# Transposes that nobody reads in TensorE's waits: a two-block model with experts on one core

## Chip, cores and metric

The kernel runs on one core of a Trainium2 chip. The metric is the device time of one execution in microseconds (us); lower is better. A profiled execution gives the trace: what each engine did and when, what ended each wait, and the clock that was granted to TensorE.

## What is computed

2048 tokens of width 1024 go through two blocks, all in float32. Cut to its steps:

```python
# first block
h = rmsnorm(x) * (1 + sc1) + sh1
q_a, k_a, v_a, q_h, f_h, i_h, g_h = split(h @ w_in)
mix = concat(window_attention(q_a, k_a, v_a), hgrn(q_h, f_h, i_h) * silu(g_h)) @ w_out
x = x + ga1 * rmsnorm(mix)
h = rmsnorm(x) * (1 + sc2) + sh2
g = top1(softmax(h @ w_rg)); e = top2(softmax(h @ w_re within g))     # 4 groups of 8 experts
y = sum over the 2 experts of weight * (silu(h @ gate) * (h @ up)) @ down
x = x + ga2 * rmsnorm(y)
# second block
xn = rmsnorm(x)
qa, ka, va, ga, qb, kb, vb, gb, iq, ik, iw, za, zb = split(xn @ w_in_2)
ya = chunked_attention(qa, ka, va, rel_bias) * silu(ga)               # 64-token chunks, 8 chunks back
yb = sparse_attention(rope(qb), rope(kb), vb, top256(index(iq, ik, iw))) * silu(gb)
out = rmsnorm(x + (sigmoid(za) * (ya @ w_branch_a) + sigmoid(zb) * (yb @ w_branch_b)) @ w_out_2)
```

## The kernel before

Every matrix product of float32 data is made from three products of halves: an operand is split into a high part (names ending in hi or h, rounded to the type float32r, mostly by ScalarE) and a low part (lo or l, the rest, by VectorE), and TensorE sums hi x hi, lo x hi and hi x lo in a PSUM bank. Activations must be transposed before that; TensorE does it by a product with an identity (`ident`) into PSUM, in groups of four 128x128 tiles in one bank.

`build` (L3062) runs five stages one after the other.

- `P1`: projections, window attention and the HGRN recurrence, to about 910 us.
- `P2` (L1127): for each of 16 blocks of 128 tokens (`unit`, L1243) the output projection (`pA`, `pS`, three products each), the two norms, the store of the new tokens to X1 and H2, 8 transposes of h, 16 router products into `pU` (tile `hT` by `wr`), and the choice of experts, a chain of small VectorE operations from the logits `lg` on. After the last block comes the table that says which tokens each expert gets (`cnt`, `order`, `base`, `gidx`; tiles `sa`, `sv`, `tab`, `perm`). To about 1168 us.
- `MoE` (L1514): 48 tiles of gathered tokens in an order written out by hand. POOL gathers four tiles ahead (`gather`, tile `xg`), `xT` transposes one, `gu` makes gate and up, `down` the rest. `W.split` splits the weights that SP's queue brings. To about 1639 us.
- `Overflow` (L1689): VectorE works out whether an expert got more tokens than the tiles hold, in `ovi`; every engine loads that value into a register (L1710) and branches on it (L1711). The body isn't run with these inputs.
- `S3` (L1858), the second block. Its first part (`run`, L2878) takes each token block in through `Combine`: POOL gathers two experts' rows (`cy`), SP loads X1 (`cx`), `finish` (L1833) weighs, sums, norms (sum of squares `css`, tile `ss`) and adds them; `norm_block` (L1949) norms again (`nss`, also `ss`), transposes and splits; and `proj` (L1988) starts the projections, 128x256 or 128x512 products into `pA`, with `rot` and `st` behind them on POOL, VectorE and ScalarE. The weights come on SP's queue into one staging buffer `ld`; ScalarE rounds them (`whi`, `whix`) and VectorE takes the rest (`wlo`). Then follow both attentions with more projections as filler, and the tail.

**What sets the order.** Except in `MoE` and `Overflow`, the program's order on each engine comes out of a plan that is made while it is built. `Clock` (L35) holds a time for each engine and each tile, with costs from formulas (`cost`, L135: a transpose 0.109 us, a gather 1.04 on POOL, and in the call 0.65 + 1.46 + 0.95 more to landing). Work is written as generators (lanes); `B.on` lets one go on once its engine and its tiles are planned to be free. `B.run` (L320) takes the first lane that can issue something, and where none can it steps the plan's time:

```python
            if state:
                idle = 0
                continue
            c.now += 0.05
            idle = idle + 1 if state is BLOCK else 0
```

The engines then run their instructions in that order, and wait for each other by semaphores. The plan isn't told how long things take on the chip. Nearly all instructions are recorded through one helper, so the trace puts them on line L122; they are told apart by their tiles. PSUM has eight banks, two for each of the names pA, pS, pT, pU; a bank is "open" in the plan from its allocation to `done`.

Of the kernel before, what the change touches and what calls it, by code (L numbers as in the profile page):

```python
# [34 lines left out]
class Clock:  # L35
# [3 lines left out]
    def __init__(self):  # L39
        self.t = dict.fromkeys(("tensor", "vector", "scalar", "gpsimd", "sync", "dma"), 0.0)  # L40
        self.ready, self.last, self.by, self.free = {}, {}, {}, {}
        self.now, self.open = 0.0, set()
# [8 lines left out]
    def op(self, eng, outs, ins, cost, lat=0.0, far=0.0):  # L51
        t = self.t[eng]
        for a in ins:
            n = a.tensor.name
            t = max(t, self.ready.get(n, 0.0) + (0.12 if self.by.get(n) != eng else 0.06))
        for a in outs:
            n = a.tensor.name
            t = max(t, self.free.get(n, 0.0))
            if self.by.get(n) != eng:
                t = max(t, self.last.get(n, 0.0))  # L60
        if eng == "sync":
            self.t[eng] = t + 0.05
            d = self.t["dma"] = max(self.t["dma"], t + 1.1) + cost
            end = d + 0.95
        else:
            self.t[eng] = t + cost
            end = t + cost + lat
            if far:
                d = self.t["dma"] = max(self.t["dma"], t + cost + 0.65) + far
                end = d + 0.95  # L70
        for a in ins:
            n = a.tensor.name
            self.last[n] = max(self.last.get(n, 0.0), end)
        for a in outs:
            n = a.tensor.name
            self.ready[n] = max(end, self.ready.get(n, 0.0)) if self.by.get(n) != eng else end
            self.last[n] = max(self.last.get(n, 0.0), end)
            self.by[n] = eng
        return t

# [127 lines left out]
class B:  # L208


    def __init__(self, tc, ctx, I):
# [4 lines left out]
        self.sm = None  # L216
        self.spawned, self.lanes = [], []
# [26 lines left out]
    def bank(self, *tags):  # L244

        while True:
            for tag in tags:
                slots = self.ps.slots.get(tag)
                if slots is None or any(x not in self.clock.open for x in slots):
                    return (yield from self.ps.get([128, 512], F32, tag, bufs=2))  # L250
            yield BLOCK

# [65 lines left out]
    def run(self, *lanes, back=(), first=()):  # L318
# [6 lines left out]
        while lanes or self.spawned:  # L325
# [15 lines left out]
            if state:  # L341
                idle = 0
                continue
            c.now += 0.05
# [782 lines left out]
class P2:  # L1127
# [336 lines left out]
    def run(self):  # L1464
        b = self.b
        st, en = b.phase("p2")
        with st:
# [3 lines left out]
            self.lg, self.perm = {}, None  # L1471
            b.run(pipe(self.units(), 4), self.mix_lane(range(4, NTB), self.P, "mraw", 2, self.P, "msq", b.rsqrt2))

# [40 lines left out]
class MoE:  # L1514
# [129 lines left out]
    def run(self):  # L1644
        st, en = self.b.phase("mo")
        with st:
            self.setup(en)
            W, NT = self.W, self.NT
            for t in range(4):
                self.gather(t)  # L1650
            W.split(3)
# [37 lines left out]
class Overflow:  # L1689
# [5 lines left out]
    def run(self):  # L1695
        b, nc, tc = self.b, self.nc, self.b.tc
        st, en = b.phase("ov")
        with st:
# [10 lines left out]
            nc.vector.tensor_copy(mi, mx)  # L1709
            v = nc.values_load(mi[0:1, 0:1], min_val=0, max_val=T)  # L1710
# [96 lines left out]
class Combine:  # L1807
# [11 lines left out]
    def block(self, blk, then=None):  # L1819
# [10 lines left out]
        yield from b.load(x, self.X1[blk * 128:blk * 128 + 128, :])  # L1830
        b.spawn(self.finish(blk, x, *ys, then))

    def finish(self, blk, x, y1, y2, then):  # L1833
# [7 lines left out]
        self.started = True  # L1841
        r = yield from b.rsqrt2(ss, 1, 1.0 / D, "cr")
# [15 lines left out]
class S3:  # L1858
# [90 lines left out]
    def norm_block(self, x, blk, hi, lo):  # L1949
# [4 lines left out]
        b.done(jk)  # L1954
        y = yield from b.rsqrt2(ss, 1, 1.0 / D, "nr")
# [885 lines left out]
    def run(self):  # L2841
# [18 lines left out]
        with self.b.pool("s_k") as c:  # L2860
            self.consts(c)
            self.keys(c)
            with ExitStack() as st:
# [4 lines left out]
                with b.pool("s_ro") as c:  # L2868
# [3 lines left out]
                    with b.pool("s_c") as self.C:  # L2872
# [4 lines left out]
                        self.W.extra, self.W.hi_eng = (self.C, range(3, 6)), "scalar"  # L2877
                        b.run(self.norm_lane(), self.proj(0, range(8), groups=True), self.const_lane(), first=b.lanes)  # L2878
                    fill = chain(self.proj(0, range(8, 32), last=True), self.xn_load(2), self.xn_load(3), self.proj(1, range(12), groups=True))
# [218 lines left out]
```

## Time and profile before

| | us |
|---|---|
| Median of 3 runs | 4056.64 |
| The runs | 4056.0, 4056.64, 4059.93 |
| Profiled execution | 4061.26 |
| Its span, first to last instruction | 4059.4 |
| TensorE (PE) busy | 3646.1 (90%) |
| VectorE (DVE) busy | 2734.8 (67%) |
| ScalarE (ACT) busy | 2283.2 (56%) |
| GpSimd (POOL) busy | 901.4 (22%) |
| Mean granted TensorE clock | 0.951 |

The trace belongs to one execution, the profiled one; 1.86 us of it lie outside the span. Times within the trace are us from the span's start. A granted clock of 1.00 is TensorE at 2.4 GHz, 0.50 is 1.2 GHz. Busy time of a matmul is from its issue to its modelled end, so neighbours overlap: in a row of like ones the distance of two starts is the price of one. PE stands for matmuls and transposes, PEld for weight loads, PEldq for the queue's own instructions, SP for the engine that issues most transfers.

### The profile page before, as it was taken

To read this page: it belongs to the slowest core of one execution; us is meant where nothing else is said; L and a number is where in the kernel's file an instruction comes from. 1 tells how busy PE (TensorE), PEld (TensorE's weight loads), DVE (VectorE), ACT (ScalarE), POOL (GpSimd) and SP (SyncE) were. 2 spreads that over 40 slices of the span, in tenths; PEclk is the share of its full clock that TensorE was granted. 3 is DMA by queue.
4 is the path that set the end of the run, shared out by engine and by line. 5 is a ranking of instruction groups with operands and counts; after the bars stand their busy time and mean duration, and the time that the engine had idled before them with its cause. 6 is when DMAs were issued, how large, how long until landed. Compare 5 with 4: busy or idle time off the path is not lost.

```text
span 4059.4 us, 64576 instructions
## 1 busy us (share of the span) xinstructions
PE 3646.1 (90%) x21649; PEld 3167.4 (78%) x21649; DVE 2734.8 (67%) x7027; ACT 2283.2 (56%) x4628; POOL 901.4 (22%) x1650
## 2 busy tenths in 40 slices
PE   3999999979969999397999989999889988999997
PEld 2888788768858888296777779888678877999997
DVE  7866785697777777526366743467766656878772
ACT  3654655565546666424257755357667774676751
POOL 1310000031011100473044526111033321211110
PEclk9999999979989999598999989999889998999999
DMA  6233451125358887739887773543166527787767
GB/s 229 79 108 110 137 198 60 64 81 167 130 202 314 314 315 285 263 126 339 290 255 249 249 283 108 169 147 101 43 187 180 173 81 270 259 281 272 265 230 283
DMA packets 425744, 801.28 MB, mean 197 GB/s; under 512 B 129360, under 2 KB 245296, under 8 KB 424496
## 3 DMA queue, kind: packets, MB, share of 16 engines
q1 hardware_dynamic: 407472, 748.70, 54.3%
q0 software_dynamic: 17920, 48.26, 3.5%
q8 instruction: 176, 2.88, 0.3%
q14 instruction: 176, 1.44, 0.1%
HBM read 571.02 MB, written 234.18 MB: 198 GB/s over the span
## 4 chain that ended last, share of the span: by engine, by line
PE 37%; DMA 7%; POOL 4%; DVE 3%; issue 3%; ACT 2%; SPq 1%; POOLq 0%; DVEq 0%; ACTq 0%
PE pA L122 22%; PE pS L122 5%; PE pT L122 5%; PE pU L122 5%; POOL rot L122 1%; DMA x<-IQ 1%; SPq L122 1%; DMA x<-QB 1%; DMA tz<-TZ 1%; POOL st L122 1%; DMA Q<-QA 0%; DMA sg<-SG 0%; DVE scb L122 0%; DVE pp L122 0%; POOL QB L122 0%
## 5 line engine op out<-in xcount | busy, mean ns | idle before, releaser
L122 PE MATMUL pA<-xnl,whi 128*128 128x512 f32 x1024 | 415.3, 406 | 5.4 <-DVE st L122 5.4
L122 DVE TENSOR_TENSOR wlo<-ld,whi 128x1024 fp32r<-128x1024 f32 x271 | 328.7, 1243 | 112.6 <-ACT whi L122 74.8
L122 PE MATMUL pA<-xnh,wlo 128*128 128x512 f32 x1024 | 403.7, 394 | 0.4 <-DVE wlo L122 0.4
L122 PE MATMUL pA<-xnh,whi 128*128 128x512 f32 x1024 | 403.9, 394 | 0.0
L122 DVE TENSOR_TENSOR pp<-pT,pp 128x256 fp32r<-128x256 f32 (+1 forms) x568 | 295.1, 537 | 117.5 <-ACT pp L122 113.8
L122 ACT ACTIVATE pp<-pT 128x256 fp32r<-128x256 f32 (+1 forms) x568 | 260.6, 478 | 201.5 <-PE pT L122 189.3
L122 PE MATMUL pA<-hlo,whi 128*128 128x512 f32 x832 | 352.1, 423 | 10.0 <-issue 6.7
L122 PE MATMUL pA<-hhi,wlo 128*128 128x512 f32 x832 | 328.8, 395 | 0.0
L122 PE MATMUL pA<-hhi,whi 128*128 128x512 f32 x832 | 327.9, 394 | 0.0
L122 ACT ACTIVATE whi<-ld 128x1024 fp32r<-128x1024 f32 x212 | 213.5, 1052 | 59.0 <-PE pA L122 35.3
L122 DVE SCALAR_TENSOR_TENSOR acc<-rl,iw,acc 128x512 f32<-128x512 f32 (+3 forms) x304 | 220.8, 727 | 38.0 <-ACT rl L122 31.4
L122 PEld LDWEIGHTS pA<-xnh,wlo 128*128 128x128 f32 x1024 | 193.9, 189 | 44.8 <-DVE wlo L122 1.1
L122 ACT ACTIVATE bias<-acc,sst 128x1152 f32<-128x1152 f32 (+13 forms) x168 | 220.0, 1309 | 13.3 <-DVE sst L122 9.6
L122 PEld LDWEIGHTS pA<-xnl,whi 128*128 128x128 f32 x1024 | 195.4, 191 | 33.6 <-issue 5.8
L122 PE MATMUL pA<-wlo,xnh 128*128 128x256 f32 (+1 forms) x672 | 200.9, 299 | 22.2 <-DVE st L122 12.4
L122 PEld LDWEIGHTS pA<-xnh,whi 128*128 128x128 f32 x1024 | 194.9, 190 | 29.4
L122 PE MATMUL pU<-pp,vbS 128*128 128x256 f32 x1088 | 203.2, 301 | 10.2 <-DVE pp L122 8.3
L122 ACT ACTIVATE rl<-pS 128x512 f32<-128x512 f32 (+3 forms) x304 | 163.6, 544 | 82.4 <-PE pS L122 42.9
L122 PE MATMUL pA<-whi,xnl 128*128 128x256 f32 (+1 forms) x672 | 197.5, 294 | 4.1 <-DMA xnl<-XND 4.1
L122 PE MATMUL pA<-whi,xnh 128*128 128x256 f32 (+1 forms) x672 | 197.6, 294 | 0.0
L122 ACT ACTIVATE st<-pA 128x256 f32<-128x256 f32 (+4 forms) x160 | 73.6, 460 | 202.6 <-PE pA L122 161.5
L122 PEld LDWEIGHTS pA<-hlo,whi 128*128 128x128 f32 x832 | 159.4, 192 | 35.9 <-issue 9.4
(494 smaller groups left out, 11117.2 us busy)
## 6 DMA issues: line engine op xcount, KB each, us to landing
whi<-W2P SPq DMA_DIRECT2D x172, 512.0 KB
wlo<-W2P SPq DMA_DIRECT2D x172, 512.0 KB
ld<-in_w_gu_dram SPq DMA_DIRECT2D x128, 512.0 KB
ld<-in_w_dn_dram SPq DMA_DIRECT2D x64, 512.0 KB
W2P<-whi SPq DMA_DIRECT2D x57, 512.0 KB
W2P<-wlo SPq DMA_DIRECT2D x57, 512.0 KB
Y<-ym SPq DMA_DIRECT2D x48, 512.0 KB
xl<-in_wadaT_dram SPq DMA_DIRECT2D x32, 512.0 KB
```

Source lines behind the costliest of these rows:

```text
L122: r = real(*a, **k)
```

## The change

While TensorE is planned to be idle it is given transposes of the identity into a PSUM bank that nobody reads. There are two kinds.

*Fixed groups*, in `turn`: 48 after the first four gathers of `MoE.run` (L1644), 56 before the register load of `Overflow.run` (L1710), and three by `turn_at` in the first token block of the second block: 56 once X1's rows have landed (`Combine.block`, L1819), 48 after the first sum of squares (`Combine.finish`, L1833) and 40 after the second (`S3.norm_block`, L1949). `turn_at` puts a one-column matmul on the tile in front, so that the group waits for it.

*Bursts of three*, in `idle_turn`: where `B.run` finds nothing to issue and steps its time, it adds three transposes if TensorE has been idle for over 0.2 us in the plan, was planned busy for less than 60% of the last stretch (`share`), and a PSUM bank is free and was last used over 0.5 us ago. This is switched on (`turning`) in `P2.run` (L1464) and in the first part of `S3.run` (L2878), which goes from about 1643 to 2000 us.

All of it enters the plan as TensorE time, so what is planned behind it may take another order.

```diff
--- before.py
+++ after.py
@@ class Clock
+        self.pe = []
...
             end = t + cost + lat
+            if eng == "tensor":
+                self.pe.append((t, t + cost))
...
+    def share(self, span=3.4):
+
+        a = self.now - span
+        while self.pe and self.pe[0][1] <= a:
+            self.pe.pop(0)
+        return sum(min(y, self.now) - max(x, a) for x, y in self.pe if x < self.now) / span
...
@@ class B
+        self.turning = False
...
+    def turn(self, n, after=None):
+
+        c, s = self.clock, self.ps.slots
+        tag = min((c.last.get(x, 0.0), tag) for tag in s for x in s[tag] if x not in c.open)[1]
+        t = yield_value(self.ps.get([128, 512], F32, tag, bufs=2))
+        if after is not None:
+            self.nc.tensor.matmul(t[:, 0:1], self.ident, after, start=True, stop=True)
+        for k in range(n):
+            self.nc.tensor.transpose(t[:, k % 4 * 128:(k % 4 + 1) * 128], self.ident, self.ident)
+        self.done(t)
+
+    def idle_turn(self):
+
+        c, s = self.clock, self.ps.slots
+        if self.turning and c.t["tensor"] < c.now - 0.2 and c.share() < 0.6:
+            if any(x is not None and x not in c.open and c.last.get(x, 0.0) < c.now - 0.5 for y in s.values() for x in y):
+                self.turn(3)
+
+    def turn_at(self, after, n):
+
+        yield from self.on("tensor", after)
+        self.turn(n, after)
+        yield 1
...
             if state:
                 idle = 0
                 continue
+            self.idle_turn()
             c.now += 0.05
...
@@ P2.run
+            b.turning = True
             b.run(pipe(self.units(), 4), self.mix_lane(range(4, NTB), self.P, "mraw", 2, self.P, "msq", b.rsqrt2))
+            b.turning = False
...
@@ MoE.run
             for t in range(4):
                 self.gather(t)
+            b = self.b
+            b.turn(48)
             W.split(3)
...
@@ Overflow.run
             nc.vector.tensor_copy(mi, mx)
+            b.turn(56)
             v = nc.values_load(mi[0:1, 0:1], min_val=0, max_val=T)
...
@@ Combine.block
         yield from b.load(x, self.X1[blk * 128:blk * 128 + 128, :])
+        if blk == 0:
+            b.spawn(b.turn_at(x[:, 0:1], 56))
         b.spawn(self.finish(blk, x, *ys, then))
...
@@ Combine.finish
         self.started = True
+        if blk == 0:
+            b.spawn(b.turn_at(ss, 48))
...
@@ S3.norm_block
         b.done(jk)
+        if blk == 0:
+            b.spawn(b.turn_at(ss, 40))
...
@@ S3.run
+                        b.turning = True
                         b.run(self.norm_lane(), self.proj(0, range(8), groups=True), self.const_lane(), first=b.lanes)
+                        b.turning = False
```

## Rows read from the trace of the kernel before

**Rows 1.** The page, part 2: granted clock in 40 slices of 101.5 us.

```profile
PEclk9999999979989999598999989999889998999999
```

**Rows 2.** Stretches: us, busy us of each engine, granted clock, DMA share, GB/s.

```profile
1142.10:1179.70 37.60, 12.46 (x53) 10.58 (x54) 25.36 (x78) 11.21 (x16) 7.92 (x5) 0.50 0.45 166
...
1179.70:1184.00 4.30, 4.30 (x20) 3.48 (x19) 4.17 (x4) 2.46 (x3) 0.00 (x0) 1.00 1.02 405
...
1640.50:1719.00 78.50, 18.09 (x78) 16.04 (x79) 49.25 (x115) 34.90 (x62) 42.15 (x36) 0.50 0.85 304
...
1740.00:1832.00 92.00, 92.00 (x782) 92.00 (x782) 19.17 (x45) 24.40 (x70) 67.62 (x246) 1.00 0.36 124
...
1841.90:1848.70 6.80, 6.20 (x29) 6.20 (x30) 5.39 (x7) 0.87 (x1) 2.37 (x1) 0.50 0.83 328
...
1864.00:1932.00 68.00, 50.10 (x298) 44.83 (x297) 41.37 (x79) 28.73 (x52) 19.98 (x12) 0.89 1.03 361
...
1938.00:2000.00 62.00, 62.00 (x283) 51.44 (x282) 17.73 (x23) 13.52 (x20) 0.00 (x0) 1.00 0.86 293
```

**Rows 3.** TensorE's timeline: start, us, operation, count, idle before and its releaser.

```profile
1124.27 0.70 PE L122 MATMUL pU<-sa,sv 128*64 128x128 f32 x8 [1.27 <-DVE sa L122]
...
1128.48 1.87 PE L122 MATMUL pU<-wr,hT 128*128 128x36 f32 x16
...
1135.75 1.03 PE L122 MATMUL pT<-ident,h 128*128 128x128 f32 x8
...
1147.31 1.94 PE L122 MATMUL pT<-ident,h 128*128 128x128 f32 x8 [8.25 <-DVE h L122]
1149.08 3.63 PE L122 MATMUL pU<-wr,hT 128*128 128x36 f32 x16
...
1164.26 1.12 PE L122 MATMUL pU<-sa,sv 128*64 128x128 f32 x8 [1.11 <-DVE sa L122]
...
1175.65 1.97 PE L122 MATMUL pT<-ident,xg 128*128 128x128 f32 x8 [9.24 <-DMA xg<-Y,gidx]
...
1638.11 0.40 PE L122 MATMUL pU<-whi,al 128*128 128x512 f32 x1
1674.99 1.94 PE L122 MATMUL pT<-ident,cx 128*128 128x128 f32 x8 [36.48 <-DVE cry L122]
```

**Rows 4.** Stretches as in rows 2: two with many transposes.

```profile
903.20:906.60 3.40, 1.54 (x9) 1.17 (x9) 3.34 (x15) 1.47 (x4) 0.00 (x0) 1.00 0.14 46
1736.00:1739.40 3.40, 1.58 (x14) 1.58 (x15) 1.91 (x2) 0.88 (x2) 3.22 (x12) 1.00 0.95 388
```

**Rows 5.** TensorE's timeline as in rows 3: the transposes there.

```profile
900.94 2.00 PE L122 MATMUL pT<-ident,sc 128*128 128x128 f32 x8
...
1737.82 1.09 PE L122 MATMUL pT<-ident,cx 128*128 128x128 f32 x8 [2.46 <-DVE cx L122]
```

**Rows 6.** VectorE's timeline: the last unit's router logits.

```profile
1152.75 0.20 DVE L122 TENSOR_TENSOR lg<-pU,rb 128x36 f32<-128x36 f32 x1 [5.59 <-PE pU L122]
```

**Rows 7.** Lines L1710 and L1711 on TensorE's queue: ns, start us.

```profile
L1710 PEldq TENSOR_LOAD <-ovi x1: 1060/1060/1060, 1640.2 to 1640.2; - x1
...
L1711 PEldq COMPARE_BRANCH  x1: 3832/3832/3832, 1641.4 to 1641.4; - x1
```

**Rows 8.** POOL's timeline: the third stage's first gather.

```profile
1646.30 0.98 POOL L122 DMA_INDIRECT cy<-Y,pos  x1 [56.77 <-DMA crow<-ROW]
```

**Rows 9.** The chain of waits, 1600 to 2020 us: start, us, what.

```profile
1823.92 9.57 DMA cy<-Y,pos
...
1842.50 7.29 PE pA L122 x36
...
1856.57 1.95 PE pT L122 x8
1858.52 6.75 PE pA L122 x42
...
1931.73 8.39 PE pA L122 x24
```

## The prediction

> **What bounds the kernel now.** I read the page first: TensorE is busy 90% of the span, and in the line of its granted clock, one digit for each 101.5 us, most are 9 (full), with a 7 in the slice from 812 us, an 8 from 1116, a 5 from 1624 and an 8 from 1827 [rows 1]. The first of these is the end of the first stage, which the change leaves alone; it bears on the other three. The change can only pay where TensorE runs at half clock (1.2 of 2.4 GHz) **and** something waits for it, so next came the table of stretches [rows 2]. The later projections are TensorE-bound at clock 1.00: 92 us busy of 92, 62 of 62. At 0.50 stand the end of the second stage (1142 to 1180, TensorE busy 12.46 of 37.60 us) and the first projections (1640 to 1719, 18.09 of 78.50), where other engines set the pace.
>
> The price of half clock is read from like operations. Eight fp32 transposes take 1.03 us at full and 1.94 at half clock [rows 3], so in a long row about 0.11 and 0.21 each (the last drains in what is over). A 128x256 matmul takes 92.00/782 = 0.118 us [rows 2] and 6.20/29 = 0.214 [rows 2].
>
> Do transposes hold the clock? At 900.94 eight of them run for 2.00 us at half clock, behind a few matmuls; from 903.20 the clock stands at 1.00. And from 1736 it stays at 1.00 over 3.4 us with 1.58 busy, most of it by 8 transposes of 1.09 [rows 4, 5]. That speaks for yes, without proving it for a stretch of transposes alone. The Trainium skill ("TensorE: Matmul & The Clock Gate", Part 4: PE-mode transpose) says the opposite: the gate "doesn't engage" for a transpose, which is not counted as busy in the same way. These rows disagree with it. By it the sum below would be not a gain but the loss of the last rival, about 25 us.
>
> **Part by part.**
>
> *Second stage, bursts of three.* Its middle is full already. In the tail the last router unit waits for its h until 1147.31, then runs 8 transposes (1.94) and 16 router matmuls (3.63) at half clock; VectorE gets lg at 1152.75 after 5.59 us of waiting for just this, and sets the chain from there [rows 3, 6]. At full clock the transposes take 1.03, as at 1135.75. The 16 have one spell at full clock beside other work, 1.87 at 1128.48 [rows 3]. So lg is 0.91 + 1.76 = 2.7 earlier at most; the copy between the two groups doesn't shrink, and I take 2.1. The eight table matmuls at 1164.26 take 1.12 against 0.70, worth 0.4; the short ones on the same chain perhaps 0.35 together. That is -2.85. Against it, a real operation can come up behind a burst: 3 x 0.109 = 0.33 us. Five handovers from VectorE to TensorE in that chain (1147, 1158, 1162, 1164, 1166), each late by 0 to 0.33, cost 0.45 on average luck. **-2.4**, between -2.85 and +1.6 (all five hit, nothing warmer).
>
> *48 before the first expert.* TensorE waits 9.24 us for the gathered tokens until 1175.65 [rows 3]. 48 x 0.11 = 5.3 us fit; then some 4 us are idle again and the clock may have fallen before the tokens land. If it holds, the eight transposes save 0.9, and the 2.1 us from their end to that of the stretch at 0.50, 1179.70 [rows 2], halve, 1.0. But the transfers run at a share of 1.02 from 1179.7 to 1184 [rows 2], where the next experts' weights come in: what is won is waited for there. At half clock 48 x 0.21 = 10.1, or 0.9 late. **0**, bounds -1.9 and +0.9.
>
> *56 before the overflow branch.* The branch isn't taken, but TensorE's queue has to pass it: it reads its register at 1640.2 and its branch takes 3.83 us, to 1645.2 [rows 7], and POOL's first gather issues at 1646.30, behind TensorE's and VectorE's queues [rows 8]. The last expert matmul starts at 1638.11 [rows 3] and ends near 1638.5, so 56 x 0.11 = 6.2 us of transposes end at 1644.7. If the queue's register load waits for the last of them, it moves from 1640.2 to 1644.7: +4.5 on all that follows. If the queue hands the transposes to the array and goes on ahead of it, the cost is 0. Before the change no matmul was outstanding at 1640.2, so no row shows which. I take **+0.8**, near the lower end, as none of the 56 waits for anything and matmuls elsewhere start back to back [rows 3], which asks for some running ahead. Ends 0 and +4.5.
>
> *First projections: 56, 48, 40 and bursts.* TensorE waits 36.48 us until 1674.99 [rows 3]. The three groups are each released by a product of the first token block's own chain, and the last, 40 x 0.11 = 4.4 us, starts some 7 us before the first real transpose, after the norm's sum of squares; it fits. At half clock it would take 8.4 and delay that transpose by about 1.5. From 1675 to 1719 matmuls at half clock are busy 18.09 of the time; VectorE's 49.25 and transfers at 0.85 set the pace [rows 2]. Warm, TensorE's share of the chain (4 transposes and a few matmuls after each norm) shortens by about 0.5. **-0.5**, ends -1.5 and +1.5.
>
> *After the TensorE-bound stretch*, bursts again. In the chain of waits stand four pieces of TensorE at half clock [rows 9]: 36 matmuls 128x256 in 7.29 us, against 36 x 0.118 = 4.25 at full clock, 3.0 to win; 8 transposes 1.95 against 1.03, 0.9; 42 matmuls 6.75 against 4.96, 1.8; 24 of 128x512 in 8.39 against 24 x 62.00/283 = 5.26 by the TensorE-bound stretch behind them [rows 2], 3.1. Together 8.8. Between 1864 and 1932 the transfers' share is 1.03 [rows 2], so what is won earlier can be waited for there. And a burst is only put where the *plan* sees TensorE idle. The plan gives a gather 1.04 + 0.65 + 1.46 + 0.95 = 4.1 us, and at 1823.92 one took 9.57 [rows 9]; the idle behind it is in part unknown to the plan. I count half: **-4.4**, ends 0 and -8.8. Bursts in front of real work, as above but over 360 us, with half of them in idle time: **+0.7**, ends 0 and +4 (a dozen at 0.33).
>
> A burst takes a PSUM bank only where one is free and old, and its transposes read only the identity: no queue of SP or POOL gets an instruction more. What changes there is the order, since every later choice of the plan follows its clocks: 2000 us of work behind this stage may come out in another order. Size and sign are open; the nearest row is the gather of 9.57 us, one slip of which on the chain is the unit. I centre it on 0, ends -6 and +10.
>
> **Sum:** -2.4 + 0 + 0.8 - 0.5 - 4.4 + 0.7 = -5.8 us. The profiled execution has 4061.26 (span 4059.4), 4.6 above the median of 4056.64; it becomes 4055.5, the median **4051**. About 0.2%, 8 us here, is what a measurement can tell from no change.
>
> **Rivals.**
>
> *All of it is won.* The bursts cover the idle as it is, the branch is free, and being early by 8.8 at 1940 stays, since 1938 to 2000 is full TensorE at 1.00: -2.85 - 1.9 - 1.5 - 8.8 = -15, so 4042. For it: pieces of TensorE at half clock lie on the chain. Against: transfers at 1.03. **0.29**, from 4036 to 4048.
>
> *Hidden.* The won time is waited for at the transfers, and the branch's drain takes 4.5: between 4050 and 4062, at 4056. **0.12**.
>
> *Another order.* A transfer of the replanned half lands a group later and TensorE waits twice the 9.57 less the 5.8 won: about +13, 4070; or the loss just eats the gain. **0.12**.
>
> *Slower, by one mechanism: transposes don't hold the clock.* It decides at the first burst after 1142. The bursts fill until 60% of a planned stretch is busy; at half clock each takes 0.64 where the plan has 0.33, so TensorE runs behind. In 1640 to 1719 some 0.6 x 78.5 - 9 = 38 planned us are filled and take 74, with 60 idle there [rows 2]: +14. In the tail 0.6 x 37.6 - 6 = 16.5 become 32, with 25 idle: +7. Add 0.9, 1.5 and the branch's 4.5 or less: **about +25**, 4082. Against it stand the rows at 900 and 1736 [rows 4, 5]; for it, that neither is a stretch of transposes alone. **0.06**. It is the case that the Trainium skill's page, above, would give.
>
> **How the numbers follow.** My own case (half the gain) has 0.41, from 4046 to 4057, and 0.12 of that lies below 4048.5. Faster by over 0.2%: 0.29 + 0.12 = 0.41. Slower: 0.06 from the clock, 0.07 from the order, 0.04 from drain plus bursts: 0.17. The rest, 0.42, is within. The range goes from the far end of the second case, 4036, to 4064, which holds all cases but the slower 0.17 and a few hundredths below it.
>
> **What would show it.** Right: clock 1.00 in the windows from 1147 to 1168, lg some 2 us earlier after h, the first gather at most 1 us later after the last expert matmul, the chain's pieces of 128x256 matmuls at 0.118 each. Wrong: a stretch filled with identity transposes at 0.50 (last rival); a load of the register at 1644 (drain); bursts of three absent from the idle before the matmuls of [rows 9], where the plan didn't see it; or a chain after 2000 whose transfers land later than before.

## The result and the profile after

The changed kernel takes **4105.16 us** (median of four runs, 4104.2 to 4105.36) against 4058.28 for the kernel before beside it: a ratio of 1.0102, 95% interval 1.0082 to 1.0122. That is 47 us slower (41 above the range's upper end, 4064), where 6 us faster had been forecast. A second measurement on another chip, among the experiments, gave 1.0109 (1.0094 to 1.0123).

The page of the changed kernel, its head and the line that answers to [rows 1]:

```profile
span 4103.5 us, 66804 instructions
...
PE 3770.0 (92%) x22767; PEld 3288.9 (80%) x22767; DVE 2729.8 (67%) x7026; ACT 2287.3 (56%) x4630; POOL 891.3 (22%) x1651
...
PEclk9999999979999999999999989999999988999999
```

TensorE got more to do (1118 instructions, 124 us) and its clock did rise: the 5 of the slice from 1624 us and the 8s from 1116 and 1827 are 9s. The span still grew from 4059.4 to 4103.5. The two stretches of [rows 2] that stood at half clock, in the changed trace (us; then busy us and instructions of PE, PEld, DVE, ACT, POOL; granted clock, DMA share, GB/s):

```profile
1142.00:1180.00 38.00, 32.49 (x236) 29.52 (x235) 28.42 (x80) 14.17 (x19) 7.93 (x5) 0.91 0.53 195
...
1640.00:1719.00 79.00, 71.75 (x625) 70.83 (x623) 50.36 (x119) 37.44 (x66) 43.05 (x43) 0.96 0.84 300
```

So with the transposes the clock is held most of the time: 0.91 and 0.96 for 0.50 and 0.50. But something else stands beside it: from 1640 to 1719 TensorE is busy 71.75 us of 79, where it was 18.09 of 78.50. The filler has made TensorE the busiest engine of a stretch in which it was the idlest.

**Where the time went.** I matched the k-th instruction of each kind in two traces and took the median lag in a stretch, less the lag at the end of the first stage (which no kernel here changes). Single executions scatter: the row of the unchanged kernel differs by up to 6 us, and its times in all measurements together run from 4052 to 4081. So over a whole stage small steps don't count, and what a kernel loses in all is taken from the medians; from one stretch to the next, where the traces of like kernels agree better, smaller steps can be read.

| lag in us behind the kernel before, at | 1228 to 1300 | 1645 | 1746 to 1800 | 1975 to 2000 | 4020 to 4055 |
|---|---|---|---|---|---|
| changed kernel | -1.2 | -2.1 | 4.9 | 9.0 | 46.7 |
| changed kernel, second chip | 2.2 | 1.3 | 8.0 | 7.6 | 48.1 |
| its plan without transposes (e1_plan_only) | 2.1 | 2.2 | 1.2 | 0.8 | 37.6 |
| the plan alone, second chip (f2_plan_only) | 2.0 | 1.1 | -0.7 | -3.2 | 27.9 |
| kernel before again (g3_before_again) | 5.5 | 5.8 | 5.2 | 4.4 | 4.0 |

Two things happen: 6 to 11 us are lost in the first part of the second block, and 38 to 40 **after 2000 us, where the change issues 30 of its 1112 transposes**; most of the second loss, 37 and 31, is there without any transposes.

**The second stage.** TensorE's timeline (start, us, operation, count; in brackets the idle time before and what ended it), answering to [rows 3], and VectorE's row for [rows 6]:

```profile
908.62 1.49 PE L132 MATMUL pA<-ident 128*128 128x128 f32 x6
...
911.18 1.11 PE L132 MATMUL pT<-ident 128*128 128x128 f32 x6
912.04 0.48 PE L132 MATMUL pA<-hlo,whi 128*128 128x512 f32 x1
...
1146.84 1.09 PE L132 MATMUL pT<-ident,h 128*128 128x128 f32 x8 [1.74 <-DVE h L132]
...
1148.42 1.87 PE L132 MATMUL pU<-wr,hT 128*128 128x36 f32 x16
...
1162.19 1.20 PE L132 MATMUL pU<-sa,sv 128*64 128x128 f32 x8
...
1173.49 1.10 PE L132 MATMUL pT<-ident,xg 128*128 128x128 f32 x8 [0.73 <-DMA xg<-Y,gidx]
...
1150.34 0.20 DVE L132 TENSOR_TENSOR lg<-pU,rb 128x36 f32<-128x36 f32 x1 [3.55 <-PE pU L132]
```

The tail does what was forecast: 1.09 and 1.87 for 1.94 and 3.63, and lg comes 3.50 us after the start of the transposes, where it came 5.44 after. But at the stage's start 18 transposes, which the plan had put into an idle time that had passed, stand **in front of** the first matmuls of `hlo` by `whi`, from 908.62 to 912.04. The 48 fill the wait for the tokens but for its last 0.73.

**The branch.** TensorE's queue at the two lines of [rows 7] (their numbers are 41 higher in the changed kernel), and POOL's timeline for [rows 8]:

```profile
L1751 PEldq TENSOR_LOAD <-ovi x1: 487/487/487, 1639.5 to 1639.5; - x1
...
L1752 PEldq COMPARE_BRANCH  x1: 6071/6071/6071, 1640.1 to 1640.1; - x1
```

```profile
1642.33 0.99 POOL L132 DMA_INDIRECT cy<-Y,pos  x1 [55.80 <-PE pA L132]
...
1662.25 2.55 POOL L132 TENSOR_TENSOR cx<-cx,cy 128x1024 f32<-128x1024 f32 x1 [12.47 <-PE pU L132]
```

TensorE's register load comes at 1639.5, 2.3 us after that of SP at 1637.2, and its branch ends only at 1646.2. The gather doesn't mind: it issues at 1642.33, 7.2 us after the start of the last expert matmul, where it took 8.2 before. What minds is TensorE itself, and behind it the add at 1662.25, which now waits 12.47 us, until a matmul ends; before, it waited 9.70 for VectorE.

**The first projections.** TensorE from the last expert matmul to the first real transposes:

```profile
1635.14 0.39 PE L132 MATMUL pU<-whi,al 128*128 128x512 f32 x1
1635.38 6.27 PE L132 MATMUL pA<-ident 128*128 128x128 f32 x56
1646.52 0.87 PE L132 MATMUL pA<-ident 128*128 128x128 f32 x3 [4.87 <-issue]
...
1661.88 0.28 PE L132 MATMUL pU<-cx,ident 128*128 128x1 f32 x2
1662.02 6.31 PE L132 MATMUL pU<-ident 128*128 128x128 f32 x56
1668.17 0.28 PE L132 MATMUL pA<-css,ident 128*128 128x1 f32 x2
1668.31 5.44 PE L132 MATMUL pA<-ident 128*128 128x128 f32 x48
1673.59 0.28 PE L132 MATMUL pS<-nss,ident 128*128 128x1 f32 x2
1673.73 4.56 PE L132 MATMUL pS<-ident 128*128 128x128 f32 x40
1678.13 1.04 PE L132 MATMUL pT<-ident,cx 128*128 128x128 f32 x8
```

From 1646.52, late from the branch, TensorE works through bursts without a gap. The first of them are at half clock (0.64 us a burst against the 0.33 of the plan), and only behind them, at 1661.88, does it reach the matmul that reads cx for the group of 56. POOL's add overwrites cx, so it waits for that matmul; the norm's groups of 48 and 40 follow, and the first real transposes start right behind the 40, at 1678.13. From the first gather that is 35.8 us; before it was 1674.99 - 1646.30 = 28.7 [rows 3, 8]. The 7.1 are the first loss. VectorE's last product on cx, which these transposes read, divides it; in the changed trace and in the one before:

```profile
1669.53 3.38 DVE L132 SCALAR_TENSOR_TENSOR cx<-cx,nry,gain 128x1024 f32<-128x1024 f32 x1
```

```profile
1671.48 3.36 DVE L122 SCALAR_TENSOR_TENSOR cx<-cx,nry,gain 128x1024 f32<-128x1024 f32 x1
```

It ends 30.6 us after the first gather, where it took 28.5: 2.0 are lost up to here, by way of POOL's add. The other 5.1 are TensorE's own: cx is ready at 1672.91, and its transposes wait behind the groups of 48 and 40.

**Behind the TensorE-bound stretch**, the chain of waits (start, us, what), answering to [rows 9], in the changed trace and in that of the second chip; under each TensorE's row of the first of the 36 matmuls:

```profile
1829.62 12.23 DMA cy<-Y,pos
...
1847.60 7.32 PE pA L132 x36
```

```profile
1847.60 0.58 PE L132 MATMUL pA<-wlo,xnh 128*128 128x256 f32 x1 [2.82 <-DVE st L132]
```

```profile
1830.52 9.83 DMA cy<-Y,pos
...
1849.37 4.60 PE pA L132 x36
```

```profile
1849.37 0.39 PE L132 MATMUL pA<-wlo,xnh 128*128 128x256 f32 x1 [0.83 <-DVE st L132]
```

In both traces the plan has put 30 transposes into the wait for the gather. In the first the gather takes 12.23 us, TensorE is idle again for 2.82, and the 36 matmuls still take 7.32, at half clock. In the second it is idle for 0.83, and they take 4.60: the gain that was forecast for them, and the lag falls from 8.0 to 3.1 by 1870.

Then bursts stand in front of real work. Between 1885 and 1895 the lag grows by 2 to 3.4 us in each of the four traces of kernels that have them there (the change twice, `e4_s3_only` and `e7_no_anchors` below), and not in the three that have the change's order without them (the plan alone twice, `e8_no_bursts`). At 2009 the last 30 transposes stand between two matmuls and cost 3.3 in the same four.

One long piece of the chain only looks like a loss. The chain in the changed trace, then VectorE and TensorE there, then both in the trace before:

```profile
1933.21 0.33 PE pS L132 x3
...
1941.40 5.51 PE pA L132 x24
```

```profile
1939.26 0.69 DVE L132 SCALAR_TENSOR_TENSOR st<-pA,st 128x512 fp32r<-128x512 f32 x1 [1.25 <-DMA KA<-st]
...
1941.16 0.49 PE L132 MATMUL pA<-xnl,whi 128*128 128x512 f32 x1
```

```profile
1930.90 0.69 DVE L122 SCALAR_TENSOR_TENSOR st<-pA,st 128x512 fp32r<-128x512 f32 x1 [1.38 <-DMA KA<-st]
...
1931.73 0.77 PE L122 MATMUL pA<-xnl,whi 128*128 128x512 f32 x1 [5.36 <-DVE st L122]
```

From 1933.21 to 1941.40 the chain consists of 8.2 us of bursts. But before, TensorE waited 5.36 us at this place, until VectorE's `st` ended. With the bursts the first of the 24 matmuls starts 1.2 us after that `st`, where it started 0.1 after it, and the 24 take 5.51 for 8.39: some 1.6 us are won.

### The profile page after: what moved, and what is told of

It is laid out like the page before. It is cut to its first block, busy times and chain, and to the rows that moved or that the text cites. A ratio compares the mean times of both kernels' runs of the same rounds, so it can differ in the third digit from the quotient of the medians.

```text
span 4103.5 us, 66804 instructions
## 1 busy us (share of the span) xinstructions
PE 3770.0 (92%) x22767; PEld 3288.9 (80%) x22767; DVE 2729.8 (67%) x7026; ACT 2287.3 (56%) x4630; POOL 891.3 (22%) x1651
## 3 DMA queue, kind: packets, MB, share of 16 engines
q14 instruction: 176, 1.43, 0.1%
## 4 chain that ended last, share of the span: by engine, by line
PE 40%; DMA 7%; DVE 4%; POOL 2%; issue 2%; ACT 2%; SPq 1%; POOLq 0%; DVEq 0%; ACTq 0%
PE pA L132 25%; PE pS L132 5%; PE pT L132 5%; PE pU L132 5%; DMA x<-IQ 2%; DMA tz<-TZ 1%; SPq L132 1%; DMA x<-QB 1%; DMA sg<-SG 1%; DMA ld<-in_w2t_dram 1%; POOL rot L132 1%; DMA wlo<-W2P 1%; DVE pp L132 1%; DMA cy<-Y,pos 1%; DVE scb L132 1%
## 5 line engine op out<-in xcount | busy, mean ns | idle before, releaser
L132 DVE SCALAR_TENSOR_TENSOR acc<-rl,iw,acc 128x512 f32<-128x512 f32 (+3 forms) x304 | 222.4, 732 | 40.4 <-ACT rl L132 33.6
L132 PEld LDWEIGHTS pA<-hlo,whi 128*128 128x128 f32 x832 | 158.5, 190 | 35.8 <-issue 9.4
```

Source lines behind the costliest of these rows:

```text
L132: r = real(*a, **k)
```

## Experiments

Theory **O**: the order loses the time. The added transposes enter the plan as TensorE time, so every later choice of the planner falls differently, and that order is worse. Theory **T**: the transposes themselves lose it, in front of real work. Both can be separated, since the plan and the instructions are two things: a transpose can be charged and not issued, or issued and not charged.

### The plan without the transposes, and the transposes without the plan

`e1_plan_only` and, on the chip of a second measurement of the change, `f2_plan_only`: `turn` charges the clock with the same times but issues nothing. VectorE, ScalarE, POOL and SP then have the changed kernel's order, instruction by instruction, and so has TensorE but for the transposes.

```diff
...
-        for k in range(n):
-            self.nc.tensor.transpose(t[:, k % 4 * 128:(k % 4 + 1) * 128], self.ident, self.ident)
...
+        for k in range(n):
+            c.pe.append((t, t + 0.109))
+            t += 0.109
+        c.t["tensor"] = t
...
```

> The plan of the changed kernel, with its order on every engine, but none of the added transposes is issued (they are only charged to the plan). Theory O (the order that the plan makes with the charged transposes loses the time; the transposes themselves gain a little): the loss stays and the clock's gain goes, 4108 to 4118 us. Theory T (the transposes themselves lose it, in front of real work and in the banks): about the time before, 4054 to 4062.

Measured: 1.0049 (1.0032 to 1.0066), 4092.36 against 4069.8, so 20 us slower (13 to 27). That lies between the two ranges: the order loses time, but not all of it.

> The changed kernel again, beside its plan without the transposes on one chip, to divide its loss. Before counts as 100%: if the order carries nearly all of it, both stand within 8 us of each other; by the traces so far (7.5 us between them in the aligned profiles, 11 lost in the first projections less what the second stage gains) it is 5 to 12 us above the plan alone. If the transposes carry half of it, 18 to 25 us above.

> The changed kernel's order without a transpose issued, on the same chip as the change: 20 to 37 us above the kernel before if the order carries most of the loss, less than 15 if the transposes do.

Measured on one chip: the change 1.0109 (1.0094 to 1.0123), 4107.51 us; its plan alone **1.0080** (1.0065 to 1.0094), 4091.27; before 4060.46. So of some 44 us the order carries 32 (26 to 38) here, and the transposes the rest, 12 with about 8 either way (16 by the medians). With the 20 of the first measurement, the order's part is somewhere from under a half to three quarters. Where the order's part is lost can be seen at one landmark, TensorE's longest wait, for the same transfer in every trace; from the kernel before, the changed one and its plan alone:

```profile
3357.97 1.09 PE L122 MATMUL pT<-ident,x 128*128 128x128 f32 x4 [26.39 <-DMA x<-QB]
```

```profile
3385.67 1.10 PE L132 MATMUL pT<-ident,x 128*128 128x128 f32 x4 [26.22 <-DMA x<-QB]
```

```profile
3379.59 1.10 PE L132 MATMUL pT<-ident,x 128*128 128x128 f32 x4 [26.75 <-DMA x<-QB]
```

The wait itself is the same, 26 us; it begins 28 and 21 us later, and the table above shows 0.8 of that lag for the plan alone at 2000. No single wait takes it: TensorE's idle time behind 2000 adds up to 150 us in the kernel before, 167 in the changed one and 171 in its plan alone, and for the changed kernel most of the rest is half clock: TensorE is busy at it for 95 us behind 2000 before and for 124 after the change, and half of the difference, 15 us, is lost. From 2400 to 2500 the mean granted clock was 0.90 before, and 0.78 in the like stretch of the changed kernel.

`e2_uncharged`, the reverse: all transposes issued, none charged; the planner's clocks are put back after each group.

```diff
+        kept = {k: dict(getattr(c, k)) for k in ("t", "ready", "last", "by", "free")}
+        c.t["tensor"] = max(c.t["tensor"], c.gt)
...
+        c.gt = c.t["tensor"]
+        for k, d in kept.items():
+            setattr(c, k, d)
```

> All the transposes of the change are issued, at the places where an idle TensorE is planned, but the plan is not charged for them, so every engine has the order of the kernel before. Theory O: faster than before, by the 4 us that the trace of the changed kernel shows up to the first gather of the second block, and by up to 9 more after it: 4045 to 4055 us. Theory T: as slow as the changed kernel, 4095 to 4110.

Measured: 1.0196 (1.0179 to 1.0213), the slowest of all. This falls on theory T's side, and more than T had asked, but the run is not a clean test: with the clocks put back the same name came out oldest time after time, so the groups went to two of the four names (741 of the 1103 transposes in its trace to pS, 362 to pA), and the plan no longer knew that TensorE was behind. Its trace shows the mechanism of T, on TensorE and POOL in the first projections:

```profile
1664.01 36.39 PE L132 MATMUL pA<-ident 128*128 128x128 f32 x114 [4.89 <-PEq L1761]
...
1701.13 2.35 POOL L132 TENSOR_TENSOR cx<-cx,cy 128x1024 f32<-128x1024 f32 x1 [33.53 <-PE pA L132]
```

114 transposes, all into pA, take 36.39 us, 0.32 each instead of 0.11 (more than the 0.21 of half clock; why, isn't shown), and POOL's add waits 33.53 us for the one matmul behind them that reads its tile. The trace says something for theory O as well: 73 us are lost by 2000, and only 7 more behind it, in the order of the kernel before. To come late to 2000 us, by itself, is not what costs the other orders their time there.

### Is the order before a lucky one?

Two kernels without any transpose, in which the plan has TensorE busy once, for 0.33 (`e6_nudge_2000`) or 0.50 us (`f4_nudge_half`), near 2000 us:

```diff
+                    b.clock.t["tensor"] = max(b.clock.t["tensor"], b.clock.now) + 0.33
                     self.chunked(0, fill, range(2, 8))
```

> The kernel before without any transpose; its plan alone has TensorE busy for 0.33 us once, at the start of the chunked attention, near 2000 us. That is enough for another order from there on. Theory O, in the form that the order before is a lucky one and any other pays: 15 to 40 us slower than before, nothing of it ahead of 2000. Rival: a nudge costs what it says, within 8 us of before; then the orders of the runs so far have something else in common.

> A second draw of an order: the kernel before without any transpose, TensorE charged with 0.50 us once near 2000 us instead of 0.33, which gives yet another order from there on. If the order before is a lucky one: 8 to 40 us slower. If orders scatter about the one before: as likely faster as slower, within 15 us.

Measured: 1.0031 (1.0016 to 1.0046) and 1.0073 (1.0056 to 1.0090), so 13 and 30 us slower, from nothing but another order; the 13 fall just short of the 15 to 40 that were expected. All the loss lies behind 2000: there the lag grows by 17 and 25 us in their traces.

`e3_no_s3` (the first diff) has the second stage's bursts, the 48 and the 56 of the change, `e4_s3_only` (the second) only what it adds to the second block; both are charged, so each has an order of its own.

```diff
-            b.spawn(b.turn_at(ss, 40))
...
-                        b.turning = True
+                        b.turning = False
                         b.run(self.norm_lane(), self.proj(0, range(8), groups=True), self.const_lane(), first=b.lanes)
```

```diff
-            b.turning = True
...
-            b.turn(48)
...
-            b.turn(56)
```

> Bursts in the second stage, 48 and 56 around the experts; nothing in the second block. The plan is charged as in the change, so the second block's order is a third one. Theory O: the first gather of the second block comes about 4 us earlier than before, and the total is off by what another order makes, either way, anywhere from 4035 to 4100, and by more than 8 us from 4054. Theory T: 4054, since the second block has no transpose in it.

> The bursts and the three anchored groups in the second block alone; second stage, experts and branch as before. Theory O: up to 1640 us as before, then again another order: 4040 to 4110, not tied to 4108. Theory T: what the second block loses in the changed kernel, about 49 us, is lost here too: 4105 to 4110.

Measured: 1.0103 (1.0085 to 1.0121) and 1.0059 (1.0042 to 1.0076). `e3_no_s3` is as slow as the whole change although nothing is added behind 1644 us; its lag is -2.6 at 2000 and 32.6 at the end. With the change and its plan that makes five orders other than that of before, and every one loses 17 to 40 us behind 2000 in its traces. (A single trace can mislead by some 10 us: the profiled execution of `h1_48_only` below, which has the order of before and nothing added behind 1180, loses 11 there, and was 9 us over its median.) That all five are worse fits an order that is better than most of its neighbours; how orders in general scatter, five draws don't tell.

### What the transposes lose in the first projections

Both keep the changed kernel's plan and order; `e7_no_anchors` doesn't issue the groups of 56, 48 and 40 in the first token block, `e8_no_bursts` doesn't issue the second block's bursts. `plan_only` charges the plan and issues nothing; the diffs in that order.

```diff
...
         yield from self.on("tensor", after)
-        self.turn(n, after)
+        self.plan_only(n, after)
```

```diff
-                        b.turning = True
+                        b.turning = "plan"
...
-                self.turn(3)
+                (self.plan_only if self.turning == "plan" else self.turn)(3)
```

> The plan and order of the changed kernel, with all its bursts and the 48 and 56; only the three groups of 56, 48 and 40 in the first token block are not issued. If those groups hold up the first block (POOL's add waits for the matmul that reads its tile, the first real transposes stand behind 40): the first real transposes come 5 to 7 us earlier than in the changed kernel and the total is 4 to 8 us below it, a ratio near 1.0088. If the bursts alone keep TensorE behind: less than 3 us.

> The plan and order of the changed kernel, with the three anchored groups, the 48 and the 56 and the second stage's bursts; only the bursts of the second block are not issued. If the bursts keep TensorE behind: the first real transposes 5 to 7 us earlier than in the changed kernel, 4 more won behind 1840, a ratio to before near 1.0080. If the anchored groups do it: less than 3 us below the changed kernel.

Measured: 1.0065 (1.0043 to 1.0088) and 1.0071 (1.0045 to 1.0096), both 13 to 18 us below the change's two ratios, from other chips. That is more than the 4 to 8 expected of the groups, and about what the change pays for transposes altogether. POOL's first gather and TensorE's first real transposes, without the groups and then without the bursts:

```profile
1644.60 0.99 POOL L132 DMA_INDIRECT cy<-Y,pos  x1 [56.10 <-DVEq L1777]
...
1674.41 1.94 PE L132 MATMUL pT<-ident,cx 128*128 128x128 f32 x8 [11.05 <-DVE cry L132]
```

```profile
1644.15 0.99 POOL L132 DMA_INDIRECT cy<-Y,pos  x1 [55.88 <-PE pA L132]
...
1652.11 0.56 PE L132 MATMUL pU<-cx,ident 128*128 128x1 f32 x2 [8.72 <-DMA cx<-X]
...
1673.38 1.15 PE L132 MATMUL pT<-ident,cx 128*128 128x128 f32 x8 [2.11 <-DVE crv L132]
```

29.8 and 29.2 us from gather to transposes, where the change has 35.8 and the kernel before 28.7. So neither of my two alternatives was right: **either kind alone fits into the wait, both together don't.** The two traces with both bear it out: 35.4 for the change on the second chip, and 33.6 for `e4_s3_only`, in which no 56 hold up the branch. The second fence shows why: without bursts ahead of it the matmul that reads cx runs at 1652.11, 8 us after the first gather; in the change it ran 19.6 after. From 1640 to 1719 (the columns of the stretches above), without the groups and then without the bursts:

```profile
1640.00:1719.00 79.00, 59.77 (x482) 58.64 (x480) 53.06 (x118) 36.97 (x66) 44.18 (x43) 0.87 0.85 312
```

```profile
1640.00:1719.00 79.00, 38.45 (x272) 36.48 (x269) 55.37 (x122) 38.85 (x69) 44.01 (x43) 0.72 0.87 321
```

TensorE is busy 59.77 and 38.45 us, not 71.75. The clock falls to 0.87 and 0.72, and these traces show no cost of that: from 1645 to 1800 the lag changes by some 2 us at most. VectorE is the busiest engine there without the bursts, as it was in [rows 2].

### The first parts alone, in the order of the kernel before

A cleaner form of issuing without charging: the banks now go round, and nothing is added to the second block. On VectorE, ScalarE, POOL and SP the order is that of the kernel before, and on TensorE too but for the transposes. `e5_before_order` has bursts, 48 and 56; `f3_tail_only` bursts in the last token block alone, 24 and 56; `g1_branch_only` the 56; `h1_48_only` the 48; `g2_tail_bursts_only` and `h2_tail_again` the last block's bursts; `g3_before_again` is the kernel before. Two lines of the diffs; the second is in those with the last block's bursts:

```diff
...
+        c.last.update({x: max(c.last.get(x, 0.0), c.gl.get(x, 0.0)) for y in s.values() for x in y})
...
+        b.turning = blk == NTB - 1
```

> The order of the kernel before on every engine; bursts in the second stage, 48 before the first expert and 56 before the branch are issued (in turn through the free banks) but not charged to the plan; no transposes in the second block. Theory O (orders lose the time, these transposes gain): faster than before by 2 to 5 us, with the first gather of the second block earlier by as much and nothing lost after it. Theory T (the transposes lose it also here): slower than before by 5 us or more.

> The order of the kernel before on every engine; uncharged bursts from the last token block of the second stage on only (so none in front of its first matmuls), 24 instead of 48 before the first expert, 56 before the branch, nothing in the second block. If what the earlier run in this order lost came from the 18 transposes at 911 us and the 48: 2 to 4 us below before at the first gather of the second block, 1 to 4 us below before in all. If bursts in the tail themselves cost: level with before or above it.

> The kernel before with nothing but the 56 transposes ahead of the overflow branch. If they help POOL's first gather as the changed trace suggests: that gather 0.8 to 1.0 us earlier against the last expert matmul, the total within 3 us of before. If they hold up the branch: the gather later, by up to 4.5 us.

> The kernel before with nothing but the uncharged bursts from the last token block of the second stage on. If the tail gains as forecast: the first transposes of an expert's tokens 2 to 3 us earlier against the first stage's end, the total 0 to 3 us below before. If a gain there is waited for again or lost behind 1640: level with before or up to 9 us above it, as in the two runs with the same order so far.

> The kernel before, unchanged, measured as the others are. Level with before, within its interval; if it comes out 5 to 9 us above, the two runs in the order before that lost as much behind 2000, where they have no transpose, lost nothing.

> The kernel before with nothing but the 48 transposes ahead of the first expert's tokens, uncharged. If they are what the two runs with all three kinds in the order before lost: 4 to 10 us slower than before, with the first expert matmuls later against the table's end. If they are hidden in the wait for the tokens: within 3 us.

> The uncharged bursts in the tail of the second stage alone, a second time and on another chip if it comes so: 2 to 8 us below before if the gain of the first time is real, within 2 us of before if it was the comparison.

| | ratio | 95% interval |
|---|---|---|
| e5_before_order: bursts, 48, 56 | 1.0015 | 1.0002 to 1.0027 |
| f3_tail_only: tail's bursts, 24, 56 | 1.0024 | 1.0013 to 1.0034 |
| g1_branch_only: 56 | 0.9997 | 0.9986 to 1.0008 |
| h1_48_only: 48 | 1.0010 | 0.9997 to 1.0022 |
| g2_tail_bursts_only | 0.9986 | 0.9975 to 0.9997 |
| h2_tail_again: the same kernel | 0.9998 | 0.9984 to 1.0011 |
| g3_before_again: nothing | 0.9995 | 0.9982 to 1.0008 |

The tail's bursts win what was forecast for them, and it is waited for again. The idle times of TensorE in `g2_tail_bursts_only` from 1170 on:

```profile
1175.11 1.94 PE L132 MATMUL pT<-ident,xg 128*128 128x128 f32 x8 [8.37 <-DMA xg<-Y,gidx]
...
1187.02 0.50 PE L132 MATMUL pA<-wlo,xh 128*128 128x512 f32 x1 [1.43 <-ACT xh L132]
...
1215.53 0.80 PE L132 MATMUL pU<-whi,al 128*128 128x512 f32 x1 [2.82 <-DVE al L132]
```

Its lag falls by 2.7 us up to the tokens' transposes and is back to where it was by 1220: 1.5 come back up to the matmul behind ScalarE's xh and 1.4 up to that behind VectorE's al. Both waits, 1.43 and 2.82, have the same size in the trace of before, so the engines ahead of TensorE set the pace there. The two measurements of this kernel, 0.14% faster and level, agree with anything from nothing to some 6 us won. The 56 move POOL's first gather 0.8 us forward against the last expert matmul and cost nothing. `e5_before_order` was to be 2 to 5 us faster and `f3_tail_only` 1 to 4; they are 6 and 10 slower. Why the three kinds together come out slower, where each alone is within 0.14%, is not settled: the intervals of the single ones are as wide as the difference, and part of it appears behind 2000, where those kernels don't differ. No version was found that beats the kernel before by more than the measurement can tell.

## Why the prediction was wrong

**"Transposes hold the clock"** was right, and more plainly than the rows it rested on: the fill raised the clock by itself (last section). It was not held everywhere: from 1160 to 1170 it is 0.66 in the changed trace, inside the stretch that was to stand at 1.00. The last rival is refuted; its sign came true by other means. The Trainium skill ("TensorE: Matmul & The Clock Gate", Part 4: PE-mode transpose) has it that a transpose doesn't count as busy for the gate; the stretch from 1652.7 to 1661.8, at 1.00 with 86 transposes and nothing else, disagrees, if the kernel's transposes run in the mode that the page means, which the trace doesn't tell.

**The step that failed first is "size and sign are open; I centre it on 0, ends -6 and +10", for the order.** It costs 32 us (26 to 38) on one chip and 20 (13 to 27) on another, with the transposes left out. I had named the mechanism, gave it 0.12 as a rival, and sized it by one slipped gather. A plan of 2000 us has no one unit: the loss is spread over many small waits and stretches of half clock. That "every later choice follows" was written in the prediction, and should have been read as a bound of its own: nothing in the trace of before says how good its order is among its neighbours, so no end of that term could be as near as +10. What was there to lose could be seen: the clock's line in [rows 1] has four more 8s, in the slices from 2334, 2842, 2943 and 3349 us, which the prediction passes over, and TensorE is idle for 150 us behind 2000.

**The step "the last, 40, fits", -0.5 with ends -1.5 and +1.5,** measured +7.1 from first gather to first transposes, 5.1 of it behind the 48 and the 40. I had costed the groups one by one against the wait of 36.48 us and never added up that queue: the plan's bursts in front of the first anchor, some 115 transposes from 1646.5 to 1661.9 and at half clock to begin with, on an engine that keeps its order, behind a branch that TensorE passes later. I had also not asked who waits for an anchor, the one-column matmul that ties a group to a tile: it reads cx, and POOL overwrites cx.

**"After the TensorE-bound stretch", -4.4, and bursts, +0.7.** The pieces were sized rightly where the bursts reached them: the 36 matmuls took 4.60 on the second chip (4.25 was the forecast), the 24 took 5.51 (5.26). In the first trace the 36 stayed at half clock, behind the gather of 12.23. What was too small is +0.7: bursts in front of real work cost 2 to 3.4 us at 1890 and 3.3 at 2009. Between 1746 and 2000 the lag grows by 4 us in the first trace and is level in the second, against the -3.7 forecast.

**"Its middle is full already"** missed the second stage's start, where 18 transposes take the 3.4 us in front of the first matmuls. What that costs can't be told: the lag at 1000 us is 1.8 and 3.3 in the two traces of the change, and 1.4 and 1.2 in those of its plan alone.

**Right in size:** lg, 1.9 earlier against 2.1; 0 for the 48, since what is won there is waited for; the eight matmuls of the table are the exception, 1.20 us for 1.12 and not the 0.7 of full clock, as they fall into the stretch at 0.66. **The branch** was right in both halves at once: TensorE's queue did come through late, by about 4 us, and with the 56 alone (`g1_branch_only`) the total didn't pay for it, as the gather didn't wait for it. With the bursts behind it, the lateness is one part of the queue in the first projections.

## What to carry to other kernels

Ahead of an in-order engine, filler is work: count it against the stretch as one queue, and ask of each piece what real instruction stands behind it and who overwrites what it reads. A piece of filler on the chain of waits isn't yet a loss: look up when the real instruction behind it could have started. Where a planner orders the program, a change that is charged to the plan is two changes; build the one without the other (charged and not issued) before believing either, and take a few nudged orders as the measure of what the plan's luck is worth. A low clock on an engine that wasn't the bound cost nothing here that could be measured.

## What was not expected of the hardware

Transposes of an fp32 identity, with nothing else on TensorE, lifted the granted clock. Two stretches of the changed trace in which TensorE runs only bursts (from 1646.5 and from 1652.7):

```profile
1646.50:1652.30 5.80, 5.78 (x27) 5.80 (x28) 0.17 (x1) 1.15 (x1) 2.67 (x3) 0.50 1.02 410
1652.70:1661.80 9.10, 9.10 (x86) 9.10 (x85) 4.98 (x9) 5.25 (x7) 0.00 (x0) 1.00 0.66 270
```

The first stands at 0.50, the second at 1.00, and between the start of the one and the end of the other TensorE ran nothing but such transposes. TensorE's queue ran ahead of its array here, but not without limit: the 56 transposes ran from 1635.38 to 1641.65, and the register load behind them came at 1639.5, 2.3 us after SP's and when some 19 were still to run.
